# A two-layer decoder trunk on one core: where layer 0's modulation dots stand, and in which tiles their weights land

## The chip, the cores and the metric

The kernel runs on one core of a Trainium2 chip. The core has a matrix engine (PE, TensorE), a vector engine (DVE, VectorE), a scalar engine (ACT), a GpSimd engine (POOL) and a queue engine (SP, SyncE) that issues most of the DMAs here. The metric is the device time of one execution in microseconds, as the median of the runs.

## The reference

Two layers; each works on x (512 tokens by 1024 features, float32) and is steered by a vector c of 1024 elements:

```python
for l in range(DEPTH):                                   # DEPTH = 2
    mod = silu(c) @ w_ada[l] + b_ada[l]                  # 1024 x 6144
    sh1, sc1, g1, sh2, sc2, g2 = split(mod, 6)
    h = rmsnorm(x, norm1_w) * (1 + sc1) + sh1
    u = h @ w_in                                         # pool, conv, q, k, v, three gates
    y_pool, y_conv, y_attn = three causal mixers of u    # y_attn: 8 heads of 64, blocks of 256
    merged = sum over i of sigmoid(gate_i) * (y_i @ p_i)
    x = x + g1 * (merged @ w_out)
    h2 = rmsnorm(x, norm2_w) * (1 + sc2) + sh2
    x = x + g2 * ((silu(h2 @ w_gate) * (h2 @ w_up)) @ w_down)
```

What the change touches is `mod`: six parts of 1024 numbers, each a product of silu(c) with a 1024 x 1024 weight, needed at six different moments of the layer. sc2 and sh2 are needed at the second norm, g1 at the first residual.

## The kernel before, in words

**The matrix products.** Features lie on the 128 partitions in KT = 8 tiles, tokens on the free axis (S = 512). Each float32 product is done as three products of shorter numbers (`mm3`: high by high, high by low, low by high), so every operand is split into a high part (`whi`, ACT, L412) and a low part (`wlo`, DVE, L415). PE walks through all products in program order. Where `mm3` is called with activations, they are `big` tiles (a pool of 46, 128 x 512 each), split by L686 (ACT) and L687 (DVE).

**The weight stream.** `fetch` (L250) brings 512 KB of packed blocks from `in_ws` into one of three `raw` tiles; ACT and DVE split them. `next_w` fetches three to four weights ahead of their use. All of it goes through SP's queue, in order: an issue that waits for its tile holds the ones behind it.

**The modulation dots.** One of the six parts is made by eight dots. For each, a transfer brings 128 x 1024 weights from `in_ada` (512 KB), and one DVE instruction (`ada_dot`, L521) multiplies them by silu(c), which lies copied on all partitions in `csil`, and sums along the row into one column of `mod`. `ada_end` (L554) adds the bias when a part's eight dots are done. `ada_step` issues the transfer (L547) and, next in DVE's order, its dot. `pin` keeps an instruction in program order.

**Turns.** After every 2048 columns of the main products (`TICK`, four 512-column groups of three products) `mm3` calls `tick`: it moves the attention's generators (`fibers`) a step, and gives `run_bulk` some credit. `bulk` is a queue of (cost, function), run as long as the credit is not negative. Layer 0's second norm's parts SC2 and SH2 (16 dots) are put into this queue when the mixers' products begin, at rate 0.33; they take `raw` tiles (`early`). Layer 0's and layer 1's first gate G1 (eight dots) is queued after `drain()`, which runs the attention to its end, at rate 1.1, in tiles called `w` (tag `w4`, six of them). G2's eight dots follow in the output projection, at rate 0.9. Layer 1's SH1, SC1, SC2 and SH2 are made elsewhere and stay as they are.

**Around it.** The attention goes by four head pairs, and each by four tiles of 128 queries (`unit`). In a unit DVE masks and reduces the scores (`pair` or `mm` tiles in PSUM), ACT takes the exponentials, DVE scales them (L825), PE transposes them, and ACT and DVE split the result into high and low (L836, L837) for the product with the values. Between these PE works on gate and projection products, whose results DVE merges (L1275 multiplies by the gate, L1290 adds; behind the attention L1312 adds, and L686 and L687 split the sum). Then the output projection starts; its first residual (L1318) needs G1. The PSUM tiles `mm` number four and are taken in turn.

Of the kernel before, what the change touches and what calls it, by code (L numbers as in the profile page):

```python
# [12 lines left out]
F32 = mybir.dt.float32  # L13
# [4 lines left out]
ALU = mybir.AluOpType  # L18
# [3 lines left out]
P = 128  # L22
D = 1024
S = 512
L = 2
KT = D // P
HEADS = 8
HD = 64
PAIRS = HEADS // 2
# [23 lines left out]
RAW, BIG = 3, 46  # L53
# [14 lines left out]
FILLERS = (2, 3)  # L68

SH1, SC1, G1, SH2, SC2, G2 = range(6)  # L70

TWO_PI = 2.0 * math.pi
RED1 = 6.28125
# [16 lines left out]
def hybrid_trunk(ctx, tc, xT, ws, ada, cols, pool_w, qk_w, crow, pos, con, out):  # L90
    nc = tc.nc
    V, A, T = nc.vector, nc.scalar, nc.tensor

    const = ctx.enter_context(tc.tile_pool(name="const", bufs=1))
    big = ctx.enter_context(tc.tile_pool(name="big", bufs=BIG))
    wp = ctx.enter_context(tc.tile_pool(name="wp", bufs=4))
# [6 lines left out]
    def nm(s):  # L103
        uid[0] += 1
        return f"{s}{uid[0]}"

    def bigt(dt=F32R):
        return big.tile([P, S], dt, tag="big", name=nm("big"))
# [4 lines left out]
    def ps_mm():  # L113
        return psum.tile([P, S], F32, tag="mm", name=nm("mm"), bufs=4)
# [4 lines left out]
    def w4(shape, dt=F32):  # L119
        return work.tile(shape, dt, tag="w4", name=nm("w4"), bufs=6)  # L120
# [8 lines left out]
    clock = [0, 0]  # L129
    fibers = []  # L130
    bulk = deque()
    bulk_rate, credit = [0.0], [0.0]

    def run_bulk(amount):
        credit[0] = min(credit[0] + amount, 4.0)
        while bulk and credit[0] >= 0:
            cost, fn = bulk.popleft()
            credit[0] -= cost
            fn()

    def flush_bulk():
        while bulk:
            bulk.popleft()[1]()

    def tick():
        for f in list(fibers):
            f[0] -= 1
            if f[0] <= 0:
                n = next(f[1], None)
                if n is None:  # L150
                    fibers.remove(f)
                else:
                    f[0] = n
        run_bulk(bulk_rate[0])

    def drain():
        while fibers:
            tick()
# [4 lines left out]
    def pin(ins):  # L163
        return tc.keep_in_program_order(ins)

    def transpose(*a):
        tc.keep_in_program_order(T.transpose(*a))  # L167

    def mm3(o, lhs, rhs, start, stop, main=True, **more):
        matmul(o, lhs[0], rhs[0], start=start, stop=False, **more)  # L170
        matmul(o, lhs[0], rhs[1], start=False, stop=False, **more)
        matmul(o, lhs[1], rhs[0], start=False, stop=stop, **more)
        if main:
            clock[0] += o.shape[-1]
            if clock[0] >= TICK:
                clock[0] -= TICK
                tick()
# [23 lines left out]
    csil = const.tile([P, D], F32, name="csil")  # L201
# [294 lines left out]
    def next_w(ahead=None):  # L496
        ahead = ahead_now[0] if ahead is None else ahead
        while at[0] < len(items) and len(loaded) <= ahead:
            loaded.append(load_w())
        return loaded.popleft()  # L500

    def wblk(w, b):
        return w[0][:, b, :], w[1][:, b, :]
# [6 lines left out]
    mod = [const.tile([P, 6, KT], F32, name=f"mod{l}") for l in range(L)]  # L510
    amod = [[const.tile([P, KT], F32, name=f"am{l}{i}") for i in range(2)] for l in range(L)]

    def fold_scale(l, i, j0, j1):
        part = SC1 if i == 0 else SC2
        nw = colt[:, l, (C_N1 if i == 0 else C_N2) + j0:(C_N1 if i == 0 else C_N2) + j1]
        V.scalar_tensor_tensor(amod[l][i][:, j0:j1], mod[l][:, part, j0:j1], 1.0, nw,
                               op0=ALU.add, op1=ALU.mult)

    def ada_dot(aw, l, part, j):

        return V.scalar_tensor_tensor(aw, aw, 1.0, csil, op0=ALU.mult, op1=ALU.mult,  # L521
                                      accum_out=mod[l][:, part, j:j + 1])
# [19 lines left out]

            pin(ins)

    def ada_step(l, part, j, early):
        aw = wp.tile([P, D], F32, tag="raw", name=nm("raw"), bufs=RAW) if early else w4([P, D])
        nc.sync.dma_start(aw, ada[l, part, j])  # L547
        with tc.issue_after(dots_after[0].ins) if dots_after[0] is not None else nullcontext():
            ins = ada_dot(aw, l, part, j)
        pin(ins)  # L550

    def ada_end(l, part):
        m = mod[l][:, part]
        V.tensor_add(m, m, colt[:, l, C_ADA + part * KT:C_ADA + (part + 1) * KT])  # L554
        if part in (SC1, SC2):
            fold_scale(l, 0 if part == SC1 else 1, 0, KT)
        if part == G1:
            V.tensor_scalar(m, m, 0.5, None, op0=ALU.mult)

    def ada_tasks(l, parts, early=False):  # L560
        out = []
        for part in parts:
            for j in range(KT):
                out.append((1.2, lambda part=part, j=j: ada_step(l, part, j, early)))
            out.append((0.2, lambda part=part: ada_end(l, part)))
        return out

# [114 lines left out]
    def split_from(src, scale=None):  # L682

        hi, lo = bigt(), bigt()
        if scale is None:
            A.activation(hi, src, AF.Copy)  # L686
            last_split[0] = V.tensor_sub(lo, src, f32(hi))  # L687
        else:
            A.activation(hi, src, AF.Copy, scale=scale)
            V.scalar_tensor_tensor(lo, src, scale, f32(hi), op0=ALU.mult, op1=ALU.subtract)  # L690
        return hi, lo
# [53 lines left out]
    def to_features(l, qk, which, hp):  # L745
        pt = ps_mm()
        for t in range(TT):
            transpose(pt[:, t * P:(t + 1) * P],
                      qk[t][:, which, 2 * hp:2 * hp + 2, :].rearrange("p h d -> p (h d)"), ident)
        return split_from(pt, scale=colt[:, l, C_QK + which:C_QK + which + 1])  # L750
# [110 lines left out]
    def start(gen):  # L861
        n = next(gen, None)
        if n is not None:
            fibers.append([n, gen])

    def attention(l, qk, v, nrq, prq, y_attn):

        for hp in range(PAIRS):
            q = to_features(l, qk, 0, hp)
            yield 1  # L870
            k = to_features(l, qk, 1, hp)
            y = bigt(), bigt()
            y_attn.append(y)
            yield 2
            for n, i in enumerate(ORDER):
                start(unit(hp, i, q, k, v, y, nrq, prq))
                yield GAP[n]
# [81 lines left out]
    for l in range(L):  # L959
# [7 lines left out]
        for n, (k, lo, hi) in enumerate([(k, 0, S) for k in range(KT)] if l == 0 else HALVES + REST):  # L967
# [20 lines left out]
            h = norm.k(k)  # L988
# [168 lines left out]
        def gate():  # L1157
            g = ps_mm()
            feature_tile(g, next_w())
            sg = bigt(F32)  # L1160
            A.activation(sg, g, AF.Tanh, scale=0.5)
            return sg

        joint = l in JOINT
# [7 lines left out]
        for j in range(2):  # L1172
            if j == 1:
                pu = ps_mm()
                feature_tile(pu, next_w())
                if joint:
                    made += [sums_one(0), sums_one(1)]
                uc[1] = bigt(F32)
                A.activation(uc[1], pu, AF.Copy)
            pc = ps_mm()  # L1180
            feature_tile(pc, next_w())
            flush_bulk()
            if joint and j == 1:
                made += [sums_one(2), sums_one(3)]
            z = bigt(F32)
            V.tensor_mul(z, pc, uc[j])
            zs.append(z)
            if not joint:
                conv_chain(j, z)
                if j == 1:  # L1190
                    bulk.append((0, lambda: pool_chain(1, pool1)))
# [42 lines left out]
        for t, src in keys_values(qk, ss, made, tables, turn) if joint else enumerate(wide()):  # L1234
            for half in range(2):
                part = src[:, half * BLOCK:(half + 1) * BLOCK].rearrange("p (n d) -> p n d", d=HD)
                o = v[half][t]
# [25 lines left out]
            y_pool.append(split_from(pp, scale=col(C_PS + j)))  # L1263

        if l == 0:
            bulk.extend(ada_tasks(l, (SC2, SH2), True))
            credit[0] = 0.0
        bulk_rate[0] = 0.33
        ahead_now[0] = 3
        if joint:  # L1270
            ready.append(gate())
# [1 line left out]
        def gated(sg, branch):  # L1273

            V.scalar_tensor_tensor(sg, sg, 1.0, branch, op0=ALU.add, op1=ALU.mult)  # L1275
# [20 lines left out]
        for step, j in GATE2:  # L1296
            if step == "gate":
                sg2[j] = gate()
                continue
            if j == 0:  # L1300
                drain()
                if joint:
                    bulk.extend(ada_tasks(l, (G1,)))
                    bulk_rate[0], credit[0] = 1.1, 0.0
            if j % 2 == 0:
                aw_ = next_w()
            p1 = ps_mm()
            for z in range(PAIRS):
                mm3(p1, wblk(aw_, 4 * (j % 2) + z), y_attn[z], z == 0, z == PAIRS - 1)
            t = sg2.pop(j)  # L1310
            gated(t, p1)
            V.tensor_add(t, t, m01[j])  # L1312
            merged.append(split_from(t))
# [158 lines left out]
        for part, (along, single, pairs) in enumerate(PARTS):  # L1472
# [36 lines left out]
            if part + 1 < len(PARTS):  # L1509
                for n in range(KT):  # L1510
                    if n == KT // 2:
                        bulk_rate[0] = 0.0
                    o = ps_mm()
# [117 lines left out]
```

## Time and profile before

| | us |
|---|---|
| median of 3 runs (1439.05 to 1442.14) | 1439.83 |
| the profiled execution | 1439.92 |
| its span | 1438.2 |
| PE busy | 1426.8 |
| DVE busy | 1060.2 |
| ACT busy | 750.2 |
| POOL busy | 162.3 |

The span is the time from the first to the last instruction on the core; the execution's own time has 1.7 us around it. A row of the timeline is: start in us, length in us, engine, line, operation, output<-input, shapes, count, and in brackets the idle time of the engine ahead of it with what ended it. SPq is SP's queue of DMA issues, PEld PE's loading of weights. A row of the table of waits is: engine and tile, what it waited for, then total, times and longest. A row of DMA issues ends with KB each and us from issue to landing (median). The granted clock is the share of full speed that PE's clock had in a stretch.

### The profile page before, as it was taken

How to read it: one execution, taken by the hardware profiler on the slowest of the kernel's cores; microseconds unless marked ns; L12 is line 12 of the kernel's file. 1: busy time of each engine (PE TensorE's matmuls, PEld its weight loads, DVE VectorE, ACT ScalarE, POOL GpSimd, SP SyncE). 2: the span in 40 equal slices, each digit the busy share in tenths (PEclk: the TensorE clock that was granted, in tenths of full speed). 3: DMA queues.
4: the chain of work that ended last, by engine and by line, in shares of the span. 5: the costliest groups of instructions: out<-in, count | busy, mean ns of one | idle time of the engine just before them, and what ended most of it. 6: DMA issues, size and time to landing. Idle time of an engine off the chain costs nothing.

```text
span 1438.2 us, 22071 instructions
## 1 busy us (share of the span) xinstructions
PE 1426.8 (99%) x8316; PEld 1256.0 (87%) x8316; DVE 1060.2 (74%) x1923; ACT 750.2 (52%) x1260; POOL 162.3 (11%) x226
## 2 busy tenths in 40 slices
PE   9999999999999999999999999999999999999998
PEld 8888887887989998989998888888889989999997
DVE  8889786678786867667789996665878747657663
ACT  6667666643554452535454675676336525435450
POOL 0111001100100210211001100011020103111200
PEclk9999999999999999999999999999999999999999
DMA  9757676786436766747627665567772537646532
GB/s 376 223 150 179 176 187 172 178 291 222 112 123 210 205 177 200 196 123 215 198 76 244 172 163 135 144 157 165 264 210 86 143 105 189 174 112 171 140 87 83
DMA packets 93707, 249.19 MB, mean 173 GB/s; under 512 B 11928, under 2 KB 24608, under 8 KB 93600
## 3 DMA queue, kind: packets, MB, share of 16 engines
q1 hardware_dynamic: 67312, 177.37, 36.4%
q0 software_dynamic: 25696, 70.27, 24.4%
q8 instruction: 65, 1.06, 0.3%
q14 instruction: 42, 0.34, 0.1%
q10 hardware_dynamic: 592, 0.14, 0.0%
HBM read 245.64 MB, written 2.10 MB: 172 GB/s over the span
## 4 chain that ended last, share of the span: by engine, by line
PE 87%; DVE 6%; DMA 3%; ACT 2%; issue 1%; SPq 0%; POOL 0%; DVEq 0%; ACTq 0%; POOLq 0%
PE mm L161 75%; PE pair L161 10%; PE mm L167 2%; DVE wlo L415 2%; DMA raw<-in_ws 1%; DVE w L521 1%; DMA w<-in_ada 1%; DMA raw<-in_ada 0%; ACT whi L412 0%; DMA w<-in_ws 0%; DMA x<-in_xT 0%; DVE big L687 0%; ACT big L686 0%; DMA tmp<-in_pool_w 0%; DVE big L1312 0%
## 5 line engine op out<-in xcount | busy, mean ns | idle before, releaser
L161 PE MATMUL mm<-big,whi 128*128 128x512 f32 (+1 forms) x4334 | 1076.2, 340 | 4.4 <-ACT big L686 1.7
L161 PEld LDWEIGHTS mm<-big,whi 128*128 128x128 f32 x4334 | 743.1, 190 | 92.7 <-issue 2.6
L161 PE MATMUL mm<-big,wlo 128*128 128x512 f32 (+1 forms) x2167 | 733.5, 338 | 0.0
L161 PEld LDWEIGHTS mm<-big,wlo 128*128 128x128 f32 x2167 | 411.9, 190 | 44.8
L412 ACT ACTIVATE whi<-raw 128x1024 fp32r<-128x1024 f32 (+2 forms) x189 | 194.9, 1033 | 185.0 <-PE mm L161 103.2
L415 DVE TENSOR_TENSOR wlo<-raw,whi 128x1024 fp32r<-128x1024 f32 (+2 forms) x189 | 222.6, 1186 | 45.8 <-ACT whi L412 45.3
L412 ACT ACTIVATE whi<-w 128x1024 fp32r<-128x1024 f32 x84 | 88.9, 1058 | 150.9 <-PE mm L161 87.3
L415 DVE TENSOR_TENSOR wlo<-w,whi 128x1024 fp32r<-128x1024 f32 x84 | 101.2, 1220 | 29.3 <-ACT whi L412 28.7
L1318 DVE SCALAR_TENSOR_TENSOR x<-mm,mod,x 128x512 f32<-128x512 f32 (+1 forms) x89 | 61.5, 694 | 75.6 <-PE mm L161 75.4
L521 DVE SCALAR_TENSOR_TENSOR w<-w,csil 128x1024 f32<-128x1024 f32 x80 | 95.8, 1219 | 14.8 <-DMA w<-in_ada 14.7
L272 POOL DMA_DIRECT2D w<-in_ws x72 | 46.6, 657 | 481.0 <-DVE wlo L415 215.6
L436 POOL DMA_DIRECT2D wlo<-in_ws x46 | 39.6, 862 | 380.1 <-ACT wlo L434 258.3
L161 PE MATMUL pair<-whi,big 128*128 128x512 f32 x256 | 82.4, 390 | 0.0
L274 POOL DMA_DIRECT2D w<-in_ws x72 | 64.9, 921 | 148.6 <-DMA w<-in_ws 148.4
L161 PE MATMUL pair<-big,whi 128*128 128x256 f32 (+1 forms) x392 | 78.9, 298 | 0.0
L161 PEld LDWEIGHTS pair<-big,whi 128*128 128x128 f32 x392 | 63.4, 191 | 2.8
L686 ACT ACTIVATE big<-big 128x512 fp32r<-128x512 f32 x52 | 32.4, 627 | 51.5 <-DVE big L1312 24.7
L432 ACT ACTIVATE whi<-raw 128x1024 fp32r<-128x1024 f32 x46 | 49.0, 1065 | 19.7 <-PE mm L161 17.0
L161 PE MATMUL pair<-big,wlo 128*128 128x256 f32 (+1 forms) x196 | 58.5, 298 | 0.0
L161 PEld LDWEIGHTS pair<-whi,big 128*128 128x128 f32 x256 | 48.1, 188 | 9.8
L161 PE MATMUL pair<-wlo,big 128*128 128x512 f32 x128 | 49.2, 390 | 0.0
L434 ACT ACTIVATE wlo<-whi 128x1024 fp32r<-128x1024 f32 x46 | 48.7, 1058 | 0.5
(235 smaller groups left out, 1409.8 us busy)
## 6 DMA issues: line engine op xcount, KB each, us to landing
raw<-in_ws SPq DMA_DIRECT2D x146, 512.0 KB, 4.3
w<-in_ada SPq DMA_DIRECT2D x80, 512.0 KB, 5.7
w<-in_ws POOLq DMA_DIRECT2D x144, 256.0 KB, 4.6
wlo<-in_ws POOLq DMA_DIRECT2D x46, 512.0 KB, 7.0
raw<-in_ws SPq DMA_DIRECT2D x64, 256.0 KB, 4.1
raw<-in_ws SPq DMA_DIRECT2D x24, 384.0 KB, 3.7
raw<-in_ada SPq DMA_DIRECT2D x16, 512.0 KB, 4.3
raw<-in_ws SPq DMA_DIRECT2D x16, 448.0 KB, 5.3
```

What stands on the lines that cost most here:

```text
L161: tc.keep_in_program_order(T.matmul(*a, **k))
L167: tc.keep_in_program_order(T.transpose(*a))
L272: nc.gpsimd.dma_start(dst, self.source(0, 1))
L274: nc.gpsimd.dma_start(dst, self.source(*other), accum_op=ALU.add)
L412: A.activation(hi[:, :n], raw[:, :n], AF.Copy)
L415: ins = V.tensor_sub(lo[:, :n], raw[:, :n], f32(hi)[:, :n])
L432: A.activation(hi[:, :n], raw[:, :n], AF.Copy)
L434: A.activation(lo[:, :n], f32(hi)[:, :n], AF.Copy, scale=-1.0)
L436: nc.gpsimd.dma_start(lo[:, i:i + m].rearrange("p b n -> p (b n)"), src, accum_op=ALU.add)
L521: return V.scalar_tensor_tensor(aw, aw, 1.0, csil, op0=ALU.mult, op1=ALU.mult, accum_out=mod[l][:, part, j:j + 1])
L686: A.activation(hi, src, AF.Copy)
L1318: V.scalar_tensor_tensor(x[k][:, lo:hi], src, mod[l][:, part, k:k + 1], x[k][:, lo:hi], op0=ALU.mult, op1=ALU.add)
```

## The change

Only layer 0's dots are touched.

- SC2 and SH2: each transfer of 512 KB becomes two of 256 KB, into two free `big` tiles; each dot becomes two of 512 columns, the second into a new small tile `modx`, which `halves_end` adds to `mod` ahead of the bias. The dots are put into a new queue, `loads`, and run three turns (DELAY) behind their transfers. The rate is 0.65 in place of 0.33.
- G1: the eight transfers are put into `bulk` when the last head pair starts, in `w4` tiles, and their dots run three turns behind. Layer 1 keeps the queueing behind `drain()`.

```diff
+SECOND = (SC2, SH2)
+DELAY = 3
...
+    loads = deque()
...
     def tick():
+        for f in loads:
+            f[0] -= 1
+        while loads and loads[0][0] <= 0:
+            loads.popleft()[1]()
         for f in list(fibers):
...
-    def ada_step(l, part, j, early):
-        aw = wp.tile([P, D], F32, tag="raw", name=nm("raw"), bufs=RAW) if early else w4([P, D])
+    modx = const.tile([P, 2, KT], F32, name="modx")
+
+    def ada_halves(l, part, j):
+        tiles = [bigt(F32) for _ in range(2)]
+        for h in range(2):
+            nc.sync.dma_start(tiles[h], ada[l, part, j][:, h * S:(h + 1) * S])
+
+        def dot():
+            for h, o in enumerate((mod[l][:, part, j:j + 1], modx[:, SECOND.index(part), j:j + 1])):
+                pin(V.scalar_tensor_tensor(tiles[h], tiles[h], 1.0, csil[:, h * S:(h + 1) * S],
+                                           op0=ALU.mult, op1=ALU.mult, accum_out=o))
+        loads.append([DELAY, dot])
+
+    def ada_later(l, part, j):
+        aw = w4([P, D])
+        nc.sync.dma_start(aw, ada[l, part, j])
+        loads.append([DELAY, lambda: pin(ada_dot(aw, l, part, j))])
+
+    def halves_end(l, part):
+        m = mod[l][:, part]
+        V.tensor_add(m, m, modx[:, SECOND.index(part)])
+        ada_end(l, part)
+
+    def ada_apart(l, parts, step, end):
+        out = []
+        for part in parts:
+            for j in range(KT):
+                out.append((1.2, lambda part=part, j=j: step(l, part, j)))
+            out.append((0, lambda part=part: loads.append([DELAY, lambda: end(l, part)])))
+        return out
...
@@ in attention(), behind the two to_features() of a head pair
+            if l == 0 and hp == PAIRS - 1:
+                bulk.extend(ada_apart(l, (G1,), ada_later, ada_end))
+                credit[0] = min(credit[0], 0.0)
...
         if l == 0:
-            bulk.extend(ada_tasks(l, (SC2, SH2), True))
+            bulk.extend(ada_apart(l, SECOND, ada_halves, halves_end))
             credit[0] = 0.0
-        bulk_rate[0] = 0.33
+        bulk_rate[0] = 0.65
...
             if j == 0:
                 drain()
-                if joint:
+                if l > 0:
                     bulk.extend(ada_tasks(l, (G1,)))
                     bulk_rate[0], credit[0] = 1.1, 0.0
```

Lines further down are numbered otherwise afterwards: L250 is L260, L415 is L425, L521 is L531, L686 and L687 are L727 and L728, L837 is L878, L1275 is L1319, L1290 is L1334, L1312 is L1356, L1318 is L1362; L560 are the transfers of halves, L564 the half dots, L570 the transfers of G1.

SP's issues, from head pair 0 on. Before, transfers of `in_ada` and of weights (`in_ws`) take `raw` tiles by turns:

```order
L547 DMA raw_1479<-in_ada 128x1024
L250 DMA raw_1515<-in_ws 128x1024
L547 DMA raw_1587<-in_ada 128x1024
L250 DMA raw_1600<-in_ws 128x1024
L250 DMA raw_1676<-in_ws 128x1024
L547 DMA raw_1723<-in_ada 128x1024
L250 DMA raw_1734<-in_ws 128x1024
```

After:

```order
L260 DMA raw_1521<-in_ws 128x1024
L260 DMA raw_1609<-in_ws 128x1024
L260 DMA raw_1691<-in_ws 128x1024
L560 DMA big_1480<-in_ada 128x512
L560 DMA big_1481<-in_ada 128x512
L560 DMA big_1509<-in_ada 128x512
L560 DMA big_1510<-in_ada 128x512
L260 DMA raw_1752<-in_ws 128x1024
```

Three weights are issued ahead of the first half now, and only weights stand in `raw` tiles.

DVE in head pair 2, round the first two tiles' softmax. Before, one dot stands right ahead of the first transposed group (`w_2433`):

```order
L521 SCALAR_TENSOR_TENSOR raw_2571,mod_116<-raw_2571,csil 128x1024
L804 TENSOR_REDUCE asm_2543<-pair_2312 128x2
L837 TENSOR_TENSOR w_2433<-mm_2428,w_2433 128x4x128
L822 TENSOR_TENSOR asm_2450<-asm_2450,asm_2457 128x2
L805 TENSOR_REDUCE asm_2545<-pair_2312 128x2
L823 RECIPROCAL asm_2450<-asm_2450 128x2
L806 TENSOR_TENSOR asm_2544<-asm_2543,nrq_829 128x2
L809 TENSOR_REDUCE asm_2538<-pair_2312 128x2
L825 TENSOR_SCALAR tmp_2451<-tmp_2451,asm_2450 128x384
L825 TENSOR_SCALAR tmp_2452<-tmp_2452,asm_2450 128x384
L837 TENSOR_TENSOR w_2478<-mm_2475,w_2478 128x2x128
```

After, two pairs stand further ahead, and none between the two groups (`w_2501`, `w_2546`):

```order
L1334 TENSOR_TENSOR big_2293<-big_2293,big_2359 128x512
L564 SCALAR_TENSOR_TENSOR big_2349,mod_116<-big_2349,csil 128x512
L564 SCALAR_TENSOR_TENSOR big_2350,modx<-big_2350,csil 128x512
L866 TENSOR_SCALAR tmp_2460<-tmp_2460,asm_2458 128x128
L564 SCALAR_TENSOR_TENSOR big_2414,mod_116<-big_2414,csil 128x512
L564 SCALAR_TENSOR_TENSOR big_2415,modx<-big_2415,csil 128x512
L846 TENSOR_REDUCE asm_2523<-pair_2372 128x2
...
L845 TENSOR_REDUCE asm_2617<-pair_2371 128x2
L878 TENSOR_TENSOR w_2501<-mm_2496,w_2501 128x4x128
L863 TENSOR_TENSOR asm_2518<-asm_2518,asm_2525 128x2
...
L878 TENSOR_TENSOR w_2546<-mm_2543,w_2546 128x2x128
L564 SCALAR_TENSOR_TENSOR big_2468,mod_116<-big_2468,csil 128x512
```

The dot next to the groups is gone; two pairs, of the parts' 13th and 14th dots, have come in at the scaling (`L866`) of the unit before it.

DVE behind the attention, where the merged sum is split for the output projection. Before, the dots of G1 (`w_...,csil`) stand among the merges (`L1275`, `L1312`) and splits (`L687`, `L415`):

```order
L687 TENSOR_TENSOR big_3357<-big_3069,big_3356 128x512
L521 SCALAR_TENSOR_TENSOR w_3367,mod_116<-w_3367,csil 128x1024
L1312 TENSOR_TENSOR big_3135<-big_3135,big_2239 128x512
L1275 SCALAR_TENSOR_TENSOR big_3241<-big_3241,mm_3388 128x512
L687 TENSOR_TENSOR big_3379<-big_3135,big_3378 128x512
L415 TENSOR_TENSOR wlo_3386<-raw_3382,whi_3384 128x1024
L1312 TENSOR_TENSOR big_3241<-big_3241,big_2412 128x512
L1275 SCALAR_TENSOR_TENSOR big_3280<-big_3280,mm_3407 128x512
L687 TENSOR_TENSOR big_3404<-big_3241,big_3403 128x512
L521 SCALAR_TENSOR_TENSOR w_3414,mod_116<-w_3414,csil 128x1024
L1312 TENSOR_TENSOR big_3280<-big_3280,big_2614 128x512
```

After, the same merges have no dot among them:

```order
L1356 TENSOR_TENSOR big_3150<-big_3150,big_2080 128x512
L1319 SCALAR_TENSOR_TENSOR big_3218<-big_3218,mm_3419 128x512
L1356 TENSOR_TENSOR big_3218<-big_3218,big_2293 128x512
L728 TENSOR_TENSOR big_3416<-big_3150,big_3415 128x512
L728 TENSOR_TENSOR big_3435<-big_3218,big_3434 128x512
L425 TENSOR_TENSOR wlo_3442<-raw_3438,whi_3440 128x1024
L1319 SCALAR_TENSOR_TENSOR big_3315<-big_3315,mm_3444 128x512
L1356 TENSOR_TENSOR big_3315<-big_3315,big_2478 128x512
L1319 SCALAR_TENSOR_TENSOR big_3348<-big_3348,mm_3463 128x512
L1356 TENSOR_TENSOR big_3348<-big_3348,big_2685 128x512
L728 TENSOR_TENSOR big_3460<-big_3315,big_3459 128x512
```

The five first dots of G2 come in a row behind these, and behind the projection's splits of weights.

More of the change, by code (lines that the diff above doesn't have):

```diff
@@ L143, in flush_bulk @@
             bulk.popleft()[1]()
+        while loads:
+            loads.popleft()[1]()
     def tick():
+        for f in loads:
+            f[0] -= 1
+        while loads and loads[0][0] <= 0:
+            loads.popleft()[1]()
         for f in list(fibers):
@@ L543, in ada_first, with ada_step @@
             pin(ins)
-    def ada_step(l, part, j, early):
-        aw = wp.tile([P, D], F32, tag="raw", name=nm("raw"), bufs=RAW) if early else w4([P, D])
+    modx = const.tile([P, 2, KT], F32, name="modx")
[23 more added lines that the diff above has]
+        return out
+    def ada_step(l, part, j):
+        aw = w4([P, D])
         nc.sync.dma_start(aw, ada[l, part, j])
@@ L558, in ada_end, with ada_tasks @@
             V.tensor_scalar(m, m, 0.5, None, op0=ALU.mult)
-    def ada_tasks(l, parts, early=False):
+    def ada_tasks(l, parts):
         out = []
@@ L563, in ada_tasks @@
             for j in range(KT):
-                out.append((1.2, lambda part=part, j=j: ada_step(l, part, j, early)))
+                out.append((1.2, lambda part=part, j=j: ada_step(l, part, j)))
             out.append((0.2, lambda part=part: ada_end(l, part)))
```

## The prediction

> **What bounds the kernel now.** I read the page's first part, then what PE waited for, then the busy time by stretches, then the order of events round the two places where PE stood still.
>
> ```profile
> PE 1426.8 (99%) x8316; PEld 1256.0 (87%) x8316; DVE 1060.2 (74%) x1923; ACT 750.2 (52%) x1260; POOL 162.3 (11%) x226
> PE mm L161 <- DVE w L837: 2.6, 2, 1.6
> PE mm L161 <- ACT big L686: 1.7, 1, 1.7
> PE mm L161 <- DVE big L687: 0.8, 1, 0.8
> ```
>
> PE is busy for 1426.8 of 1438.2 us, so only 11.4 us are open to any change that leaves its products alone, and this one does. The waits (us in total, times, longest) show where nearly half of that lies: two waits for L837, one for L686, one for L687, together 5.1 us. All four are in layer 0, in the stretch that the change rewrites. In the next rows (window, length, then busy time and rows of PE, PEld, DVE, ACT, POOL, then the granted clock, the DMA share and GB/s) the same work stands for layer 0 and layer 1, then the microseconds behind the two stops.
>
> ```profile
> 138.00:385.00 247.00, 241.89 (x1239) 201.30 (x1238) 183.31 (x427) 133.98 (x266) 24.18 (x30) 0.99 0.70 193
> 848.00:1090.00 242.00, 242.00 (x1260) 203.69 (x1257) 166.63 (x394) 135.69 (x269) 25.05 (x31) 1.00 0.64 168
> 239.00:240.00 1.00, 0.54 (x1) 0.50 (x2) 0.90 (x6) 0.00 (x0) 0.00 (x0) 0.52 0.93 332
> 240.00:241.00 1.00, 1.00 (x4) 0.75 (x3) 0.96 (x4) 0.00 (x0) 0.00 (x0) 0.50 1.14 315
> 241.00:242.00 1.00, 1.00 (x4) 0.81 (x3) 0.74 (x3) 0.17 (x1) 0.00 (x0) 0.50 0.80 152
> 242.00:243.00 1.00, 1.00 (x4) 0.79 (x4) 0.58 (x1) 0.14 (x1) 0.00 (x0) 0.77 1.03 213
> 341.00:342.00 1.00, 0.88 (x3) 0.74 (x4) 1.00 (x2) 0.47 (x3) 0.00 (x0) 0.72 0.33 78
> 342.00:343.00 1.00, 1.00 (x4) 0.81 (x3) 1.00 (x2) 0.81 (x1) 0.00 (x0) 0.50 0.91 332
> 343.00:344.00 1.00, 1.00 (x3) 0.73 (x3) 1.00 (x3) 0.00 (x0) 0.00 (x0) 0.50 0.77 205
> 344.00:345.00 1.00, 1.00 (x4) 0.79 (x3) 1.00 (x3) 0.00 (x0) 0.00 (x0) 0.57 0.92 266
> ```
>
> Layer 1 carries its dots without a single PE gap; layer 0 has 5.1 us of gaps, and behind each a phase in which the granted clock is half: (0.28 + 0.50 + 0.50 + 0.43)/0.5 = 3.4 us by the last four rows. Such a phase loses busy time x (1 - clock): 0.26 + 0.50 + 0.50 + 0.23 = 1.5 us at the first and 0.25 + 0.50 + 0.50 + 0.43 = 1.7 us at the second. So a stop costs its idle time and some 1.6 us more.
>
> **The first stop (stop A, head pair 2).** In the order of time, with the idle time of the engine and its releaser in brackets:
>
> ```profile
> 226.52 1.22 DVE L521 SCALAR_TENSOR_TENSOR raw<-raw,csil 128x1024 f32<-128x1024 f32 x1
> 227.78 0.33 SPq L547 DMA_DIRECT2D raw<-in_ada  x1
> 234.58 1.23 DVE L521 SCALAR_TENSOR_TENSOR raw<-raw,csil 128x1024 f32<-128x1024 f32 x1 [4.96 <-DMA raw<-in_ada]
> 236.34 0.68 DVE L837 TENSOR_TENSOR w<-mm,w 128x512 fp32r<-128x512 f32 x1
> 238.99 0.41 DVE L837 TENSOR_TENSOR w<-mm,w 128x256 fp32r<-128x256 f32 x1
> 237.07 0.74 PE L161 MATMUL mm<-w,big 128*128 128x256 f32 x4 [0.93 <-DVE w L837]
> 239.46 1.22 PE L161 MATMUL mm<-big,whi 128*128 128x512 f32 x2 [1.65 <-DVE w L837]
> ```
>
> The transfer needs the `raw` tile that the dot of 226.52 leaves, so it is issued only at 227.78; its own dot, next in the order of DVE, holds DVE for 4.96 us; the two L837 behind it (the low parts of transposed probabilities: PE multiplies them with the values, and needs the PSUM slots that they read) come late, and PE stops for 0.93 + 1.65 = 2.58 us. With the clock: 4.1 us.
>
> **The second stop (stop B, output projection of the mixers' sum).** The first two rows are DVE's dots alone (window, length, busy, rows: two rows to a dot, itself and its accumulator's reading) between the attention's end and the stop, and in the same stretch of layer 1.
>
> ```profile
> 296.00:341.00 45.00, 14.62 (x24) 1.00 0.80 269
> 1003.00:1047.00 44.00, 9.64 (x16) 1.00 0.72 252
> 337.22 1.22 DVE L521 SCALAR_TENSOR_TENSOR w<-w,csil 128x1024 f32<-128x1024 f32 x1
> 339.25 1.22 DVE L415 TENSOR_TENSOR wlo<-raw,whi 128x1024 fp32r<-128x1024 f32 x1
> 340.38 0.68 DVE L687 TENSOR_TENSOR big<-big,big 128x512 fp32r<-128x512 f32 x1
> 339.77 0.50 PE L161 MATMUL mm<-big,whi 128*128 128x512 f32 x1 [1.68 <-ACT big L686]
> 341.12 0.54 PE L161 MATMUL mm<-big,whi 128*128 128x512 f32 x1 [0.84 <-DVE big L687]
> ```
>
> Layer 0 carries 12 dots here, layer 1 eight, and layer 1 doesn't stop. DVE is late at the last merges and splits of the sum, whose products PE has reached: 1.68 + 0.84 = 2.52 us idle, with the clock 4.2 us.
>
> **The change, part by part.**
>
> *Second norm's 16 dots.* Out of the `raw` tiles: no transfer waits for a tile that a weight holds, and no weight for one that a dot holds. Each dot is queued three turns behind its transfer. A turn is 12 products of 512 columns. The next rows give its length, the prices of the transfers, and the leads and margins used below.
>
> ```profile
> 195.76 0.63 PE L161 MATMUL mm<-big,whi 128*128 128x512 f32 x2
> 196.46 0.62 PE L161 MATMUL mm<-big,whi 128*128 128x512 f32 x2
> raw<-in_ada SPq DMA_DIRECT2D x16, 512.0 KB, 4.3
> raw<-in_ws SPq DMA_DIRECT2D x64, 256.0 KB, 4.1
> w<-in_ada SPq DMA_DIRECT2D x80, 512.0 KB, 5.7
> 240.18 0.68 DVE L1275 SCALAR_TENSOR_TENSOR big<-big,mm 128x512 f32<-128x512 f32 x1
> 240.78 0.41 DVE L852 TENSOR_TENSOR tmp<-tmp,mm 64x256 f32<-64x256 f32 x1
> 213.22 0.28 DVE L859 TENSOR_TENSOR big<-tmp,big 128x128 fp32r<-128x128 f32 x1
> 219.16 0.29 DVE L859 TENSOR_TENSOR big<-tmp,big 128x128 fp32r<-128x128 f32 x1 [1.02 <-ACT big L858]
> 194.60 0.41 DVE L837 TENSOR_TENSOR w<-mm,w 128x256 fp32r<-128x256 f32 x1
> ```
>
> Three products take 0.70 us (195.76 to 196.46), so a turn is 2.8 and three turns 8.4 us, twice the 4.1 to 4.3 us that such a transfer takes to land: the wait of 4.96 us at stop A has no cause left. Gain: 4.1 us. *Halves instead of a whole:* a 512-wide operation of the same kind is listed with 0.68 us, the next starts 0.60 behind it; two take 1.2 to 1.4 us where the whole dot took 1.22. For 16 dots that is nothing to 3 us of DVE time, beside PE's work while DVE has gaps: 183.3 us busy of 247 now. Cost 0; if the cover is gone, it is the third rival. *16 more issues on SP*, 0.33 us each (the row at 227.78): 5.3 us on a queue that issues and waits, nothing else. What is late on it is seen at the weights; these are issued from their own three tiles, none of them lent to dots. Cost 0. *The wider rate* (0.65 for 0.33) puts all 16 dots ahead of head pair 3's scores; now, in the order of DVE, 12 stand ahead of the attention's end and four behind it.
>
> *First gate's eight dots.* They leave the stretch of stop B: three or four of them are still between the attention's last product and the first merges, none stands between the merges, where twelve and their transfers stood. DVE loses at least eight dots of 1.22 = 9.8 us there, against a delay of 2.5. Gain: 4.2 us. The five dots of G2 that now stand in a row behind the projection stand so in layer 1 too, behind its own projection. The price is in head pair 3, where two dots now stand in the chain of softmax; layer 1 has no such pair, so it is bounded: 0, if the slack of the chain takes 2.4 us, to one stop like A, 4.1. I take 0, the nearest row being the dot of 191.47 in head pair 1, which stands inside the same chain in the kernel before without a stop:
>
> ```profile
> 191.47 1.21 DVE L521 SCALAR_TENSOR_TENSOR raw<-raw,csil 128x1024 f32<-128x1024 f32 x1
> PE mm L161 <- DVE wlo L415: 0.4, 1, 0.4
> ```
>
> *The rest.* `halves_end` adds one 8-column addition per part, among DVE's smallest operations. I allow one new short wait of PE of 0.4 us, the size of the one small wait for DVE that the table has elsewhere.
>
> **Sum.** 1439.92 (the profiled execution, 0.09 above the median of the runs) - 4.1 - 4.2 + 0.4 = 1432.0 us. A second way, from the two layers: layer 0's 1239 rows at layer 1's pace are 1239 x 242/1260 = 238.0 us, 9.0 under the 247 that they take; so no more than about 9 can be won, 1430.9, and with the noise of such counting 1429.5.
>
> [...]
>
> **Rivals.**
> 1. *The stop moves instead of going.* The second transfer of the 12th pair goes into the tile that the 11th dot leaves. That dot stands directly behind the L859 of 213.22, its pair behind that of 219.16: a lead of about 5 us, not 8.4, against 4.1 to 4.3 to land, 5.7 beside heavier traffic. Pairs 13 and 14 stand almost back to back just ahead of the chain of head pair 2. A late landing would hold DVE at stop A's place, for 1 to 4.1 us: 1433.0 to 1436.1. Against it: DVE is idle for 4.96 us there now, and those two pairs take 2.8.
> 2. *It does nothing that counts*: stop B stays, because splits and merges alone overfill DVE, 1439.92 - 4.1 + 0.4 = 1436.2; with a new stop in A's place 1440.3. For it: L415 takes 1.22 at 339.25 in the last chain. Against it: layer 1's stretch, with eight dots more, has no stop.
> 3. *Slower: DVE is late inside the softmax chains.* At 195.01 (194.60 + 0.41) L837 gives back the slot that PE takes at 195.76: 0.75 us to spare. In the new order a dot or a pair stands between two L837 in head pairs 0, 1 and 3. If each puts L837 back by its own 1.2 to 1.4 us and what waits behind it, up to stop A's price, that is 3 x 4.1 = 12.3: 1439.9 - 8.3 + 12.3 = 1443.9. From 2.8 us a place it takes the whole gain, from 3.8 it is slower by more than can be missed. Against it: in head pair 1 the dot of 191.47 stands between them now, and PE runs on.
> 4. *The half-clock phases aren't the stops' doing*, and come anyway: only the idle time goes, 1439.92 - 5.1 + 0.4 = 1435.2. Against it: 242 us of layer 1 without a gap have the clock at 1.00. [...]
>
> **Chances.** The forecast has 0.71 (its own range 1429.5 to 1433), the first rival 0.11, the second 0.09, the third 0.06, the fourth 0.03. A measurement tells 0.2%, 2.9 us, from no change; so faster means under 1436.9: the forecast, the first and the fourth rival, 0.85 less a little for the first's far end, 0.84; same 0.10; slower 0.06. The range goes from 1429.5 to 1437.0 and takes in the first and the fourth rival.
>
> **What would show it.** Of the changed kernel: no wait of PE for what L837 and L686 are called there (L878, L727), granted clock 1.00 in every 10-us window between head pair 0 and the second norm, the same 247 us of work in about 239. Each half dot at 0.6 to 0.7 us, without a wait for a transfer. Wrong, if PE waits for the probabilities' low parts in head pair 2 (first rival) or in the three others (third), or if DVE stays busy without a gap up to the projection's last merge (second).

## The result, and the profile after

The changed kernel takes 1429.81 us (median of 4 runs, 1429.64 to 1430.85) where the kernel before takes 1439.62 in the same measurement (1439.05 to 1442.14): ratio 0.993, 95% interval 0.9913 to 0.9947. The forecast was 1432.0 with a range from 1429.5 to 1437.0: right in its direction, 2.2 us too high, inside the range near its lower end. The profiled execution took 1429.94 us, its span 1428.2.

The page's first line, the largest waits of PE, and the stretches that answer to those shown of before (window, length, busy time and rows of PE, PEld, DVE, ACT, POOL, then clock, DMA share, GB/s):

```profile
PE 1422.3 (100%) x8316; PEld 1254.4 (88%) x8316; DVE 1060.9 (74%) x1957; ACT 750.6 (53%) x1260; POOL 162.7 (11%) x226
PE pair L171 <- POOL ones L228: 1.1, 1, 1.1
PE mm L177 <- ACT wlo L444: 0.4, 1, 0.4
PE mm L171 <- ACT big L899: 0.2, 1, 0.2
138.00:377.00 239.00, 238.42 (x1243) 200.04 (x1242) 184.58 (x462) 133.88 (x266) 24.22 (x30) 1.00 0.71 199
330.00:340.00 10.00, 10.00 (x45) 8.29 (x45) 9.97 (x16) 3.83 (x6) 1.13 (x2) 1.00 0.51 170
```

The four waits of 5.1 us are gone; the 1.1 us at the program's start stays. From 138 us on the same work takes 239 us where it took 247, at a clock of 1.00. In 330 to 340 DVE is busy for 9.97 of 10.00 us, and PE runs on all the same: the last split of the merged sum has started at 331.2 (340.38 in the kernel before), and what DVE does behind it delays no product there. How busy DVE is says nothing here (9.66 us in the same window of the kernel before, where PE is busy for 8.32), what it is busy with does.

PE's instructions come in the same order in both kernels, so each can be set beside itself. Its start in the two traces (us):

| PE instruction, by its place in the order | before | after | gained so far |
|---|---|---|---|
| 1148, right ahead of stop A | 235.76 | 235.44 | 0.32 |
| 1165, behind it and its slow clock | 243.70 | 239.15 | 4.55 |
| 1474, ahead of stop B | 302.24 | 298.08 | 4.16 |
| 1640, behind it and its slow clock | 344.87 | 335.95 | 8.92 |
| 4583, layer 1 | 807.85 | 798.37 | 9.48 |

Stop A gave 4.23 us (4.55 - 0.32) and stop B 4.76 (8.92 - 4.16). A new short wait right ahead of 1474 (0.19 us in the row, for `big` of L899) took 0.4 back; 0.56 more came in layer 1, where the wait of 0.4 us for `wlo` didn't recur. The wait of 0.4 us near 160 us, for `wlo` of L444, was made up again ahead of 1148. The spans differ by 10.0.

At stop A's place, SP's issue of the 14th and 15th pairs' transfers, the two half dots of the 14th, and the two L878 behind them:

```profile
220.42 2.08 SPq L560 DMA_DIRECT2D big<-in_ada  x4
227.99 0.68 DVE L564 SCALAR_TENSOR_TENSOR big<-big,csil 128x512 f32<-128x512 f32 x1
228.63 0.69 DVE L564 SCALAR_TENSOR_TENSOR big<-big,csil 128x512 f32<-128x512 f32 x1
232.54 0.69 DVE L878 TENSOR_TENSOR w<-mm,w 128x512 fp32r<-128x512 f32 x1 [0.75 <-ACT w L877]
235.83 0.41 DVE L878 TENSOR_TENSOR w<-mm,w 128x256 fp32r<-128x256 f32 x1
```

DVE goes through the 13th and the 14th pair without a wait and is at the two L878 some 3 to 4 us earlier than before (236.34 and 238.99). It was close: of the 14th pair the trace has the halves landing at 227.86 and 228.60, and their dots start at 227.99 and 228.63. The transfers themselves cost more than forecast:

```profile
w<-in_ada SPq DMA_DIRECT2D x80, 512.0 KB, 5.6
big<-in_ada SPq DMA_DIRECT2D x32, 256.0 KB, 7.0
138.00:377.00 239.00, 20.89 (x64) 1.00 0.71 199
```

A half of 256 KB takes 7.0 us to land in the median. The last row is the half dots alone: 20.89 us for 16 pairs with their 32 readings of the accumulator, 1.4 more than the 19.5 that 16 whole dots take (32 dots with readings were 38.91 us in the same stretch of before); within the bounds of 0 to 3.

### The profile page after: what moved, and what is told of

Same layout as the page of the kernel before. It is cut to its first block, busy times and chain, and to the rows that moved or that the text cites. A ratio compares the mean times of both kernels' runs of the same rounds, so it can differ in the third digit from the quotient of the medians.

```text
span 1428.2 us, 22139 instructions
## 1 busy us (share of the span) xinstructions
PE 1422.3 (100%) x8316; PEld 1254.4 (88%) x8316; DVE 1060.9 (74%) x1957; ACT 750.6 (53%) x1260; POOL 162.7 (11%) x226
## 4 chain that ended last, share of the span: by engine, by line
PE 97%; DVE 1%; ACT 1%; DMA 0%; issue 0%; SPq 0%; POOL 0%; DVEq 0%; ACTq 0%; POOLq 0%
PE mm L171 82%; PE pair L171 13%; PE mm L177 2%; DMA tmp<-in_pool_w 0%; DVE wlo L425 0%; ACT whi L442 0%; SPq L1154 0%; ACT wlo L444 0%; DVE big L1174 0%; DVE w L1254 0%; ACT L752 0%; DVE big L1284 0%; ACT whi L422 0%; ACT tmp L765 0%; DVE tmp L782 0%
## 5 line engine op out<-in xcount | busy, mean ns | idle before, releaser
L425 DVE TENSOR_TENSOR wlo<-raw,whi 128x1024 fp32r<-128x1024 f32 (+2 forms) x189 | 222.4, 1186 | 44.0 <-ACT whi L422 41.1
L425 DVE TENSOR_TENSOR wlo<-w,whi 128x1024 fp32r<-128x1024 f32 x84 | 101.2, 1220 | 28.8 <-ACT whi L422 28.0
L1362 DVE SCALAR_TENSOR_TENSOR x<-mm,mod,x 128x512 f32<-128x512 f32 (+1 forms) x89 | 61.5, 693 | 75.9 <-PE mm L171 75.7
L531 DVE SCALAR_TENSOR_TENSOR w<-w,csil 128x1024 f32<-128x1024 f32 x80 | 95.6, 1219 | 13.4 <-DMA w<-in_ada 13.2
L727 ACT ACTIVATE big<-big 128x512 fp32r<-128x512 f32 x52 | 32.4, 627 | 38.7 <-DVE big L1356 12.6
L444 ACT ACTIVATE wlo<-whi 128x1024 fp32r<-128x1024 f32 x46 | 48.6, 1057 | 0.5
```

The source lines that it names most:

```text
L425: ins = V.tensor_sub(lo[:, :n], raw[:, :n], f32(hi)[:, :n])
L444: A.activation(lo[:, :n], f32(hi)[:, :n], AF.Copy, scale=-1.0)
L1362: V.scalar_tensor_tensor(x[k][:, lo:hi], src, mod[l][:, part, k:k + 1], x[k][:, lo:hi], op0=ALU.mult, op1=ALU.add)
```

## The experiments

Each run stands beside runs of the kernel before on the same chip; the ratios are to those. Two factors were moved apart first: the second norm's part and the first gate's.

**The second norm's part alone.** In the changed kernel, G1 goes back behind `drain()`:

```diff
-            if l == 0 and hp == PAIRS - 1:
-                bulk.extend(ada_apart(l, (G1,), ada_later, ada_end))
-                credit[0] = min(credit[0], 0.0)
...
-                if l > 0:
+                if joint:
                     bulk.extend(ada_tasks(l, (G1,)))
```

> Second norm's part alone: SC2 and SH2 in halves as in the changed kernel; G1's eight dots of layer 0 queued behind the drain, as before. Theory 1 (stop B was too many dots at once, twelve; layer 1 stands eight): both stops are gone, 1430 to 1431, no wait of PE over 0.5 us between 300 and 345. Theory 2 (stop B comes from G1's dots among the merges as such): stop B stays with 2.5 us idle and its half-clock phase, 1434 to 1435.

Measured: 1430.15 us (1429.26 to 1430.43), ratio 0.994 (0.9927 to 0.9952): both stops are gone without G1's move. Dots alone in 45 us from the attention's end on (window, length, DVE busy, rows), then the last of G1's dots, the last splits of the merged sum, the first dot of G2, and PE's longest wait but that at the program's start:

```profile
292.00:337.00 45.00, 12.99 (x21) 1.00 0.71 240
317.79 1.22 DVE L531 SCALAR_TENSOR_TENSOR w<-w,csil 128x1024 f32<-128x1024 f32 x1
330.06 1.42 DVE L728 TENSOR_TENSOR big<-big,big 128x512 fp32r<-128x512 f32 x2
333.66 1.22 DVE L531 SCALAR_TENSOR_TENSOR w<-w,csil 128x1024 f32<-128x1024 f32 x1
PE mm L177 <- DVE tmp L895: 0.4, 1, 0.4
```

The window's 12.99 us look like the 14.62 of before, but they aren't the same dots: from 333.66 on they are G2's, behind the last split, where they can't delay it. Between DVE's last row of the attention and the last split there are eight dots here, G1's, and eleven in the kernel before: three of SH2's first (303.5, 307.4, 311.9), then G1's eight, four of them among the last merges (322.8, 327.8, 331.0, 337.2); the twelfth of the prediction's window, at 297.3, stands ahead of that row. Here G1's are through at 319, since nothing stands ahead of them in the queue; from 320 to 333 DVE has merges and splits alone. Eight dots don't stop PE here (no wait over 0.4 us), as in layer 1 of the kernel before (busy for 242.00 of 242.00 us).

**The first gate's part alone.** The second norm's dots as before (raw tiles; `ada_raw` issues the transfer and, next, its dot; rate 0.33), G1 ahead of what is left of them when head pair 3 starts:

```diff
...
-            bulk.extend(ada_apart(l, SECOND, ada_halves, halves_end))
+            bulk.extend(ada_tasks(l, SECOND, ada_raw))
...
-        bulk_rate[0] = 0.65
+        bulk_rate[0] = 0.33
...
-                bulk.extend(ada_apart(l, (G1,), ada_later, ada_end))
+                bulk.extendleft(reversed(ada_apart(l, (G1,), ada_later, ada_end)))
+                bulk_rate[0] = 0.65
```

> First gate's part alone: G1's eight dots beside head pair 3, ahead of what is left of the second norm's; SC2 and SH2 in raw tiles with the dot in the transfer's own step, rate 0.33 up to head pair 3 and 0.65 from there. The order up to head pair 3 is that of before, so both theories expect stop A (2.6 us idle, 4.3 us in all). Nine dots are left between 296 and 341, where twelve stood. Theory 1 (the number counts): stop B gone or under 0.5 us idle, 1435 to 1436. Rival (the seven raw tiles that dots now share with the projection's weights make a new wait for a weight): 1437 to 1441.

Measured: 1436.66 us (1435.54 to 1439.31), ratio 0.9983 (0.9974 to 0.9991). The waits of PE at stop A and B, the clock behind A, then a late dot in a raw tile, the issue of a weight behind it, and DVE's wait for that weight:

```profile
PE mm L171 <- DVE w L885: 3.0, 2, 1.6
PE mm L171 <- ACT big L734: 1.2, 1, 1.2
240.00:250.00 10.00, 10.00 (x39) 8.09 (x39) 5.89 (x17) 4.69 (x14) 0.00 (x0) 0.76 0.31 64
315.55 1.22 DVE L531 SCALAR_TENSOR_TENSOR raw<-raw,csil 128x1024 f32<-128x1024 f32 x1
316.81 0.33 SPq L260 DMA_DIRECT2D raw<-in_ws  x1
321.42 1.23 DVE L425 TENSOR_TENSOR wlo<-raw,whi 128x1024 fp32r<-128x1024 f32 x1 [4.64 <-ACT whi L422]
```

Stop A is there in full (L885 is L837). Stop B is half gone: 1.2 + 0.2 us idle and no slow clock, though there are only eight dots between the attention and the last split (340.48), as many as in the run before, which had no stop. What is new is the wait of 4.64 us: the second norm's late dots share the raw tiles with the projection's weights; the weight in question is issued at 316.81, right behind the end of a dot in a raw tile (315.55 to 316.70), and DVE stands still until it has landed and ACT has made its high part. So both theories of the expectation are seen in part, and the time lies between theirs. G1's move is worth 2.5 us of the 9.8 here, with the other half missing.

**Which of tile, delay and rate does it.** Three runs take one of them back from the changed kernel, one puts the rate alone into the kernel before. No delay (`dot()` called in the transfer's step, with halves in free tiles):

```diff
-        loads.append([DELAY, dot])
+        dot()
```

> The changed kernel, but each pair of half dots stands in DVE's order at its transfer's step and not three turns (8.4 us) behind. The leads from issue to dot in the changed kernel's profile, 5.9 to 22 us, less 8.4: three or four pairs (4th, 12th, 14th) would have 6 to 8 us too little. Theory 1 (the delay does it): DVE waits for three or four transfers, two or three stops of 3 to 4 us, 1437 to 1442. Rival (the free tiles do it, since SP runs ahead of the order and the tiles have long been free): 1429.5 to 1431.

Measured: 1441.00 us (1436.97 to 1445.27), ratio 1.0014 (1.0004 to 1.0024).

```profile
DVE big L564 <- DMA big<-in_ada: 10.4, 7, 2.4
PE mm L171 <- DVE w L878: 2.9, 2, 2.0
PE mm L177 <- DVE tmp L866: 2.1, 1, 2.1
PE mm L171 <- DVE big L1319: 1.9, 2, 1.0
170.00:180.00 10.00, 8.61 (x31) 6.73 (x32) 7.57 (x18) 2.19 (x4) 0.00 (x0) 0.66 0.65 202
```

Seven waits for halves, none over 2.4 us, and PE stops six times for 0.8 to 2.1 us, once with a slow clock. The whole gain is lost. The theory held, the mechanism was spread wider than expected: many short waits, not three or four of 6 to 8 us.

The delay with the weights in raw tiles as wholes:

```diff
+    def ada_raw(l, part, j):
+        aw = wp.tile([P, D], F32, tag="raw", name=nm("raw"), bufs=RAW)
+        nc.sync.dma_start(aw, ada[l, part, j])
+        loads.append([DELAY, lambda: pin(ada_dot(aw, l, part, j))])
...
-            bulk.extend(ada_apart(l, SECOND, ada_halves, halves_end))
+            bulk.extend(ada_apart(l, SECOND, ada_raw, ada_end))
```

> The changed kernel, but SC2's and SH2's weights come as wholes of 512 KB into the three raw tiles that the weight stream uses; the dots stay three turns behind. Theory 1 (the sharing of tiles does the harm): a raw tile is held 8 us longer, so weights and the next dots' transfers are issued late; DVE or PE waits for them, 1436 to 1450. Rival (the delay alone is what helped): 1429.5 to 1431.

Measured: 1441.74 us (1439.02 to 1443.27), ratio 1.0018 (1.0009 to 1.0027).

```profile
194.24 0.33 SPq L260 DMA_DIRECT2D raw<-in_ws  x1
200.11 1.06 ACT L442 ACTIVATE whi<-raw 128x1024 fp32r<-128x1024 f32 x1 [4.86 <-DMA raw<-in_ws]
ACT whi L442 <- DMA raw<-in_ws: 16.8, 8, 5.1
PE mm L177 <- DVE tmp L900: 3.1, 2, 2.3
PE mm L171 <- DVE w L883: 3.0, 3, 1.9
```

Here it is the weights that come late, eight times in this line alone: one is issued at 194.24, ACT waits 4.86 us for it, and with it the chain of softmax that ACT serves. Delay without free tiles gave nothing.

The rate alone, 0.65, in the kernel before:

```diff
-        bulk_rate[0] = 0.33
+        bulk_rate[0] = 0.65
```

> The kernel before with nothing changed but the rate, 0.65 for 0.33: raw tiles, each dot in its transfer's own step, more of them ahead of the attention's end. Theory 1: twice the places where a transfer waits for the tile that the dot just before leaves, so stop A comes two to four times, stop B goes; 1440 to 1446. Rival (the rate alone is the change, tiles and delay do nothing): 1430 to 1432.

Measured: 1445.04 us (1443.63 to 1448.71), ratio 1.0042 (1.0028 to 1.0056).

```profile
PE mm L167 <- DVE tmp L854: 5.2, 4, 1.9
PE mm L161 <- DVE w L837: 3.2, 2, 2.7
ACT whi L432 <- DMA raw<-in_ws: 15.9, 6, 3.5
```

PE stands still for 8.4 us in these two lines; stop B is gone (no wait for L686 or L687 is listed), with eight dots behind the attention. The expected time came, but not in the expected way: no wait of a dot for its transfer is listed here. It is the weights again that come late, and ACT waits for them, 15.9 us in the third line. The rate is what clears stop B, and on its own it costs more than it gives.

The reverse, the second norm's part alone at the old rate (free tiles and delay kept, the diff above with its sign turned, in the kernel of the first experiment):

> The run with the second norm's part alone, but at the old rate, 0.33: free tiles, halves, three turns of delay, G1 as before, and again eleven dots between the attention's end and the last merge (three pairs of halves, eight of G1). Theory 1 (stop B is the number of dots that lie there): stop A gone, stop B back, 4 us or a little less above that run, 1433.5 to 1435. Rival (stop B was the late transfers into raw tiles shared with the projection's weights): both gone, 1430 to 1431.

Measured: 1432.01 us (1430.76 to 1433.11), ratio 0.9948 (0.9935 to 0.996). PE's waits at stop B, the stretch of it, and one of the G1 dots that stand among the last merges again (327.3 and 330.2):

```profile
PE mm L171 <- ACT big L727: 0.6, 1, 0.6
PE mm L171 <- DVE big L728: 0.5, 2, 0.2
330.00:340.00 10.00, 8.80 (x35) 6.21 (x34) 9.28 (x17) 3.70 (x5) 0.00 (x0) 1.00 0.63 215
330.23 1.22 DVE L531 SCALAR_TENSOR_TENSOR w<-w,csil 128x1024 f32<-128x1024 f32 x1
```

Stop A is gone at the old rate too. Stop B is back, with eleven dots again (three pairs of halves and G1's eight), but at 1.2 us idle (10.00 - 8.80) and with the clock at 1.00: 1.9 us above the first experiment by the medians, 1.2 by the ratios, whose intervals overlap, where 4 were expected. That the stop comes back with the three late dots is shown by the rows; that its price would be that of before was a miss.

**How much delay.** One turn instead of three, for the halves and for G1's dots:

```diff
-DELAY = 3
+DELAY = 1
```

> The changed kernel with all delays of one turn, 2.8 us, in place of three. Leads from issue to dot fall by 5.6 us: the 4th pair (lead 10.9, landed 8.6 after issue) and the 14th (7.6, 7.5) would be 3 to 5.5 us short, the 12th (5.9, 3.3) 3. Theory 1 (each turn of delay counts): one or two stops, 1433 to 1439. Rival (one turn is enough, it only takes the dot off the transfer's own step): 1429.5 to 1431.

Measured: 1436.00 us (1433.25 to 1437.92), ratio 0.9974 (0.9963 to 0.9986).

```profile
DVE big L564 <- DMA big<-in_ada: 5.9, 5, 1.8
DVE w L531 <- DMA w<-in_ada: 5.6, 3, 2.8
PE mm L177 <- DVE tmp L895: 2.0, 2, 1.2
```

5.9 us of waiting for halves, 10.4 without delay, none in the changed kernel with three turns; 5.6 more here for G1's whole tiles. The time goes the same way: 1441.0, 1436.0, 1429.8.

**What is left.** A floor that leaves out layer 0's transfers and dots of SC2, SH2 and G1:

> A floor: the changed kernel without layer 0's 24 transfers and dots of SC2, SH2 and G1 (these parts are set to zero plus bias; the output isn't the reference's). Theory 1 (all dots of the changed kernel lie beside PE's work, but for short waits of 0.4 and 0.2 us): 1429 to 1430, no difference from the changed kernel that can be measured. Rival (DMA traffic or DVE load still cost PE something that the waits don't show): 1424 to 1428.

Measured: 1428.95 us (1428.92 to 1429.78), ratio 0.9928 (0.9916 to 0.994), not to be told from the changed kernel by its interval. The transfers and dots of 24 weights of 512 KB are hidden all but completely. One short wait stands even here (0.9 us for `L1300`, a place outside the change).

The rate between the two:

```diff
-        bulk_rate[0] = 0.65
+        bulk_rate[0] = 0.5
```

> The changed kernel at rate 0.5 for 0.65: the 13th and 14th pair no longer stand back to back, five G1 dots are left behind the attention. Room over the floor without dots is 0.9 us. Theory 1 (only two small waits are left, of 0.4 and 0.2 us, and no stop comes with up to eight dots behind the attention): 1429 to 1430.2, not to be told from the changed kernel. Rival (five dots among the merges are too many already): 1431 to 1434.

Measured: 1428.70 us (1428.19 to 1429.18), ratio 0.9927 (0.9913 to 0.9941), against 1429.93 for the run after this one on the same chip, the changed kernel with layer 1's G1 moved too. Of PE's waits only these are left, three of them outside the change:

```profile
PE pair L171 <- POOL ones L228: 1.1, 1, 1.1
PE pair L171 <- ACT ccol L931: 0.3, 1, 0.3
PE mm L171 <- ACT big L899: 0.2, 1, 0.2
PE mm L171 <- ACT big L713: 0.2, 1, 0.2
```

The wait of 0.4 us near 160 us is gone, with the dots further apart. Five of G1's dots stand behind the attention, one of them at 329.79, right ahead of the last split (330.9), and PE doesn't stop: a dot among the last merges is not enough by itself. It is the best version run, at the floor. It beats the kernel before clearly, and the changed kernel by medians (1.1 us) whose intervals of the ratio overlap.

Layer 1's G1 moved in the same way, in the changed kernel (`if hp == PAIRS - 1:` without `l == 0`, and no queueing behind `drain()`):

> The changed kernel with layer 1's G1 moved beside its last head pair in the same way. Layer 1 has no stop and eight dots behind its attention. Theory 1 (moving G1's dots is worth nothing where they don't stop PE): 1429.5 to 1430.5, no difference. Rival (less DVE load behind the attention also shortens what follows): 1427 to 1429.

Measured: 1429.93 us (1429.32 to 1430.11), ratio 0.9934 (0.9922 to 0.9946): no difference. Where dots didn't stop PE, moving them was worth nothing here (1429.81 us without the move).

**Were the two stops chance?** The kernel before again:

> The kernel before once more, for a second profile. Theory 1 (both stops belong to the order of the instructions): the same two stops at the same places, 2 to 3 us idle each with a half-clock phase behind; the single wait of 0.4 us for a weight's low part in layer 1, which the runs since don't show at that place, may be gone. Rival (they were this one execution's chance): one of them missing, 1434 to 1436.

```profile
PE mm L161 <- DVE w L837: 2.6, 2, 1.7
PE mm L161 <- ACT big L686: 2.4, 2, 1.7
PE mm L161 <- DVE big L687: 1.1, 2, 0.8
```

Both stops recur, stop B larger (3.5 us idle for 2.5); its one execution took 1441.62 us. The wait of 0.4 us for a low part in layer 1 is gone, so this part of the difference was chance.

## Why the prediction was right, point by point

*What bounds the kernel, and stop A.* Right, and shown: the transfer of the 9th dot into the tile that the 8th leaves. The runs add that it took both, tile and distance. At the rate of 0.65, neither gave 1445.0 us (with G1 as before), free tiles alone 1441.0, distance alone 1441.7, both 1429.8; at the old rate neither gave 1439.8 and both 1432.0, with stop A gone. Whether halves are better than wholes in free tiles, no run shows. The prediction took 4.1 us for a half to land, from weights of the same size; with the 7.0 that it measured, three turns are just enough, one is not.

*Stop B.* The amount was nearly right, the cause half wrong. The prediction laid 4.2 us to the first gate's move. With the second norm's part in place that move is worth 0.3 us by the medians (1430.15 against 1429.81) and 1.4 by the ratios (0.994 against 0.993), whose intervals overlap, so nothing that these runs can tell; without it 2.5. The step that failed is "DVE loses at least eight dots of 1.22 = 9.8 us there", as the price of clearing the stop: the first experiment loses three of eleven, 3.7 us, and the stop with them. The rate takes them away, which the prediction names among the second norm's parts without giving it a share of the gain. Layer 1's eight dots without a stop, quoted in the prediction, had said so. Dots between DVE's last row of the attention and the last split, counted in each trace, and PE's idle time at that place:

| run | dots | PE idle, us |
|---|---|---|
| before; before again | 11; 11 | 2.5; 3.5 |
| second norm alone, old rate | 11 | 1.2 |
| first gate alone (DVE waits 4.6 us for a weight) | 8 | 1.4 |
| second norm alone; before at the doubled rate | 8; 8 | 0; 0 |
| changed, rate 0.5 | 5 | 0 |
| changed | 2 | 0 |

Their number fits every run, if the wait for the weight is counted with it; no run changes the order alone. That the total held is luck in part: both halves of the change were made together, so that it didn't show which of them the 4.2 us belonged to.

*The sum.* Forecast 8.3 for the stops, measured 9.0 (4.23 + 4.76). The idle time by the busy rows is short for three of the four waits: by the starts of PE's products, beside the changed kernel's, stop A's waits are 1.09 and 1.65 us, where the rows have 0.93 and 1.65, and stop B's 1.85 and 1.12, where they have 1.68 and 0.84. A product is listed with 0.39 us but the next follows after 0.23 (three in 0.70 us at 195.76 in the kernel before), so that some of the waiting is counted as busy. The four make 0.6 of the missing 0.7. The allowance of 0.4 for a new short wait was right in size (the 0.4 ahead of product 1474), and 0.56 came back by chance in layer 1. The second estimate, from layer 1's pace, said 9.0 and was the better one.

*The halves, 16 more issues, the rate's density.* Cost nothing that can be measured, by the floor (1428.95 us without these dots, 1429.81 with them). The halves did land later, not earlier, than wholes (7.0 us in the median against 5.6 for the wholes of the other parts).

*The rivals.* The first was near: 0.03 us between the landing of the 14th pair's second half and its dot; it named the 12th as the tight one, which had 2.5 us left. Its mechanism is what the run with one turn of delay shows. The second and third didn't occur. The fear behind the third, DVE late inside the softmax chains, is seen in the kernel before at the doubled rate, at 1445.0, but there by late weights. The fourth, that the slow clock would come anyway, is refuted here: the clock is at 1.00 from 138 to 377 us, where PE has none of the two stops.

## What to carry to other kernels

A dot that waits for its data held everything behind it on its engine (DVE for 4.96 us at stop A): put it a landing time behind its transfer (7.0 us here, in the median) *and* give the transfer a tile that no weight and no neighbour holds, since either alone gave nothing here (1441.0 and 1441.7 us, against 1429.8 with both). When work in a queue delays PE at the end of a stretch, count what stands ahead of the last step, and leave out of the count what stands behind it: eleven dots stopped PE here (1.2 to 3.5 us idle), eight did not (0 us, where no weight was late). An earlier start of the first job took three away and the stop with them, and moving the other eight as well was worth nothing that could be told (1430.15 us without, 1429.81 with). Two layers that do the same work are a good ruler: the pace of the undisturbed one gave the gain better (9.0 us) than the sum of the waits (8.3), where the two stops gave 9.0.

## What the runs showed of the hardware that was not expected

The same amount of idle time cost PE's clock once and not another time. With 0.93 + 1.65 us idle (the kernel before, stop A) and 1.36 + 1.65 (first gate alone, ahead of the same two products) the granted clock fell, to 0.50 for 3.42 us in the first, to 0.76 over ten microseconds in the second; with 0.49 + 2.72 ahead of the same two products of the kernel before at the doubled rate it stayed at 1.00. The two half-clock phases of the kernel before (window, length, PE's busy time and rows, the granted clock, DMA share, GB/s), then PE's two gaps at the doubled rate, the stretch that they stand in (busy time of all engines) and the stretch behind it (of PE alone):

```profile
239.04:242.46 3.42, 3.00 (x7) 0.50 0.97 260
341.44:344.86 3.42, 3.42 (x9) 0.50 0.80 237
245.66 0.74 PE L161 MATMUL mm<-w,big 128*128 128x256 f32 x4 [0.49 <-DVE w L837]
249.12 0.73 PE L161 MATMUL mm<-big,whi 128*128 128x512 f32 x2 [2.72 <-DVE w L837]
240.00:250.00 10.00, 6.78 (x32) 5.18 (x31) 5.09 (x11) 6.77 (x14) 0.86 (x1) 1.00 0.62 185
250.00:260.00 10.00, 10.00 (x50) 1.00 0.82 204
```

With the clock at half a product follows the one before it after 0.43 us (341.46 and 341.89 in the kernel before), where it is 0.23 at full clock (345.10 and 345.33). By busy time x (1 - clock), an estimate from the first two rows, 3.00 x 0.50 = 1.5 us behind stop A and 3.42 x 0.50 = 1.7 us behind stop B hang on that. In these three places neither the longest gap goes with it (1.65 us twice with a fall, 2.72 without) nor the sum of the two (2.58 and 3.01 us with a fall, 3.21 without). What decides it is not shown here.
